# A fused Mamba/MLP mixer layer: the last quarter of the shift and scale sum moved from TensorE to VectorE, and h written by ScalarE

## The chip, the core and the metric

The kernel runs on one core of a Trainium2 chip. The metric is the device time of one execution in microseconds (us); lower is better. The kernel before takes 989.76 us, the median of three runs (989.73 to 990.02).

## The reference

The layer mixes 256 latent tokens, after 256 context tokens, in a width of 2048. What matters here is its beginning: two vectors of conditions, `c` for the latent tokens and `c_ctx` for the context, are multiplied by the large matrix `w_ada`, and the results shift and scale the normalised tokens ahead of the input projection.

```python
sc = jax.nn.silu(c); scc = jax.nn.silu(c_ctx)
shift, scale, gate = jnp.split(sc @ w_ada[l] + b_ada[l], 3, axis=-1)
shift_c, scale_c, gate_c = jnp.split(scc @ w_ada[l] + b_ada[l], 3, axis=-1)
hc = _rmsnorm(ctx, g_pre[l]) * (1.0 + scale_c) + shift_c
zc = hc @ w_in[l][:, :XBC_W + DT_W]
hx = _rmsnorm(x, g_pre[l]) * (1.0 + scale[:, None]) + shift[:, None]
zx = hx @ w_in[l]
```

Everything after that (a convolution, two state-space scans, a gated MLP, the output projection) is the same in both kernels.

## The kernel before, in words

The 2048 channels are 16 tiles of 128 partitions, and `xT` holds all 512 tokens (256 context, 256 latent) along the free axis. h, the normalised, scaled and shifted input, is needed as two halves, `hhi` (rounded to TensorE's fp32r format) and `hlo` (the rest), and each weight likewise as `hi_st` and `lo_st`; a product then takes three matmuls (`mm3`, lines 141 to 143).

**The first stage** ends at about 130 us. It runs 16 rows, one for each channel tile `kt` (line 451). Row `kt` multiplies h of tile `kt` by the weights of seven output tiles and of dt, and sums into PSUM banks that stay open over all rows. A row begins with the matmul of `psdt` by `hhi` (line 418); its fourth matmul group needs `hlo`. While TensorE runs row `kt`, the other engines make what row `kt`+1 needs: the weights' halves (`split_hi` on ScalarE, L352; `split_dt` and `split_lo` on VectorE, L356 and L360) and h itself.

**Shift and scale.** `w_ada` comes in chunks of 1 MB. Tiles 0 to 3 are single units of two chunks; tiles 4 to 15 are six units of two tiles and four chunks each. For a unit `ada_mm` runs 16 matmuls of 128 columns a chunk (L249), in exact fp32, which the profile shows as two records a matmul, so 128 records for four chunks. `ada_fin` transposes the sum (VectorE, L257), and `ada_ab` makes ha = (1 + scale) g and hb = shift, four numbers a partition (ScalarE, L262 and L264).

**h.** `make_h` works on 128x256 halves, context and latent apart: VectorE multiplies x by ha and by `rb`, the row of 1/rms (L365, two instructions), ScalarE adds hb and rounds into `hhi` (L368, two), VectorE forms `hlo` (L370, two).

**What sets the order.** Loads go out on SP's queue in program order; chunks take six buffers in turn, so the load of chunk c+6 waits for the reader of chunk c. The order of TensorE, VectorE, ScalarE and GpSimd in this stage is written by hand: `row_steps` returns a list of steps for a row ("m" a group of matmuls, "a" a chunk, "f" `ada_fin`, "h" `make_h`, "c", "d", "l" the three parts of the weights' split), and each engine runs its instructions in that order. From row 6 on, an odd row ends with h of the next tile behind "f", and an even row begins with the splits and h of the next.

**Ahead of the rows** the sum of x squared for the 1/rms is formed as the four loads of x land: ScalarE and VectorE square tiles in turn (L315, L313), TensorE sums them (L317), with matmuls on ones between them that fill time (`warm`, L305). The sum is transposed (L325), becomes `rb` (L333), and row 0 follows.

Of the kernel before, what the change touches and what calls it, by code (L numbers as in the profile page):

```python
# [15 lines left out]
P = 128  # L16
# [12 lines left out]
NSING = 4  # L29

# [14 lines left out]
def tile_hybrid_ssd_mlp(  # L45
# [66 lines left out]
    def tri(pool, name, sgn, strict):  # L112
# [69 lines left out]
    nc.sync.dma_start(sc2, ccols)  # L182

# [49 lines left out]
    def ada_one(u):  # L233
        pt = ada_ps.pop(u)[1]
        nc.scalar.activation(ha[:, u, :], pt[:, 0:2], AF.Identity, bias=bsc1[:, u : u + 1],
                             scale=pc[:, C_GPRE + u : C_GPRE + u + 1])
        nc.scalar.activation(hb[:, u, :], pt[:, 2:4], AF.Identity, bias=pc[:, C_BADA + u : C_BADA + u + 1])

    def ada_mm(ci):
# [5 lines left out]
        for kk in range(nk):  # L245
            k = k0 + kk
            for g in range(4):
                o = (kk * 4 + g) * n
                nc.tensor.matmul(ps[32 * g : 32 * g + 32, 0:n], lhsT=sc[:, k, :], rhs=raw[:, o : o + n],  # L249
                                 start=k == 0, stop=k == KT - 1)  # L250

    def ada_fin(u):

        ps = ada_ps.pop(u)
        n = 64 * len(UNITS[u])
        ada_ps[u] = tr = st2.tile([P, 128], F32, tag="row", name=f"adat{u}")
        nc.vector.transpose(tr[:, 0:n], ps[:, 0:n])  # L257
        ada_ab(u, 0)

    def ada_ab(u, q):  # L260
        kt, tr = UNITS[u][q], ada_ps[u]
        nc.scalar.activation(ha[:, kt, :], tr[:, 64 * q : 64 * q + 2], AF.Identity, bias=bsc1[:, kt : kt + 1],  # L262
                             scale=pc[:, C_GPRE + kt : C_GPRE + kt + 1])
        nc.scalar.activation(hb[:, kt, :], tr[:, 64 * q + 32 : 64 * q + 34], AF.Identity,  # L264
                             bias=pc[:, C_BADA + kt : C_BADA + kt + 1])
# [31 lines left out]
    nc.scalar.activation(sc[:, :, 0:2], sc2, AF.Silu)  # L297
    nc.scalar.activation(sc2[:, 0, 0:1], epsc, AF.Sqrt)
# [11 lines left out]
    for k in range(KT):  # L310
        sq = yseg((1, 2, 3, 6, 0, 4, 5)[k % 7])
# [6 lines left out]
        if g == 3:  # L318
            warm(512)
            if k < 12:  # L320
                warm(256)
# [39 lines left out]

    def make_h(kt):
        sl = (slice(256, 512), slice(0, 256))
        for v, s in enumerate(sl):
            nc.vector.scalar_tensor_tensor(xT[:, kt, s], xT[:, kt, s], ha[:, kt, v : v + 1], rb[:, s],  # L365
                                           op0=ALU.mult, op1=ALU.mult)
        for v, s in enumerate(sl):
            nc.scalar.activation(hhi[kt][:, s], xT[:, kt, s], AF.Identity, bias=hb[:, kt, v : v + 1])  # L368
        for v, s in enumerate(sl):
            nc.vector.scalar_tensor_tensor(hlo[kt][:, s], xT[:, kt, s], hb[:, kt, v : v + 1],  # L370
                                           hhi[kt][:, s].bitcast(F32), op0=ALU.add, op1=ALU.subtract)
# [9 lines left out]
    def row_steps(kt):  # L381
# [10 lines left out]
        s_ = [("c", n), ("d", n), ("l", n)]  # L392

        a = [("a", c) for c in range(2 * kt + 2, min(2 * kt + 6, 2 * KT))] if n >= NSING and kt % 2 else []
        f = [("f", (n - NSING) // 2 + NSING)] if kt % 2 else []
        f2 = [("f2", (n - NSING) // 2 + NSING)] if kt % 2 else []
        c_, d_, l_, h_ = s_ + [("h", n)]
        if n < NSING:
            r = [("r", 2 * n), ("r", 2 * n + 1)]
            g = m[4:5] + [("g", n), ("o", n), h_]  # L400
            if n < 3:
# [927 lines left out]
```

## Time and profile before

| what | value |
|---|---|
| median of three runs | 989.76 us (989.73 to 990.02) |
| profiled execution, span from first to last instruction | 987.9 us |
| TensorE matmuls busy over the span | 978.8 us, 99% |
| VectorE busy | 621.4 us, 63% |
| ScalarE busy | 495.4 us, 50% |
| granted TensorE clock, mean | 0.999 |
| data moved | 207.26 MB, 210 GB/s over the span |

The profiled execution's span is 1.9 us shorter than the median time of the runs; the rest lies around the span. A profile row of a group reads: line, engine, operation, output<-inputs, shapes, count | busy us, mean ns of one | idle before and what ended it. A row of the timeline reads: start, us, engine, line, operation, shapes, count, and in brackets how long the engine sat idle before it and what ended that. Line numbers in profile rows are those of the kernel before.

### The profile page before, as it was taken

How to read it: one execution, taken by the hardware profiler on the slowest of the kernel's cores; microseconds unless marked ns; L12 is line 12 of the kernel's file. 1: busy time of each engine (PE TensorE's matmuls, PEld its weight loads, DVE VectorE, ACT ScalarE, POOL GpSimd, SP SyncE). 2: the span in 40 equal slices, each digit the busy share in tenths (PEclk: the TensorE clock that was granted, in tenths of full speed). 3: DMA queues.
4: the chain of work that ended last, by engine and by line, in shares of the span. 5: the costliest groups of instructions: out<-in, count | busy, mean ns of one | idle time of the engine just before them, and what ended most of it. 6: DMA issues, size and time to landing. Idle time of an engine off the chain costs nothing.

```text
span 987.9 us, 13929 instructions
## 1 busy us (share of the span) xinstructions
PE 978.8 (99%) x5502; PEld 792.6 (80%) x5502; DVE 621.4 (63%) x949; ACT 495.4 (50%) x762; POOL 112.5 (11%) x162
## 2 busy tenths in 40 slices
PE   9999999999999999999999999999999999999997
PEld 4688888778887878787888888887888888888885
DVE  4444488868886566756767766767555564445636
ACT  4233358566665554545445343454565563346522
POOL 0000002432453222224000000000000000000000
PEclk9999999999999999999999999999999999999999
DMA  9999844233323424145877768774455446556722
GB/s 372 421 418 418 352 149 166 86 129 128 128 75 139 142 98 145 43 169 206 297 302 284 275 257 296 280 274 170 170 180 203 171 170 213 178 206 228 282 86 85
DMA packets 31985, 207.26 MB, mean 210 GB/s; under 512 B 4128, under 2 KB 4384, under 8 KB 8496
## 3 DMA queue, kind: packets, MB, share of 16 engines
q1 hardware_dynamic: 29232, 192.79, 52.0%
q0 software_dynamic: 2112, 12.65, 3.7%
q8 instruction: 43, 0.70, 0.3%
q10 hardware_dynamic: 576, 0.94, 0.3%
q14 instruction: 22, 0.18, 0.1%
HBM read 204.20 MB, written 2.16 MB: 209 GB/s over the span
## 4 chain that ended last, share of the span: by engine, by line
PE 92%; DMA 4%; ACT 2%; DVE 1%; SPq 0%; issue 0%; ACTq 0%
PE pa L1108 12%; PE pa L1110 12%; PE pa L1109 12%; PE psx L141 9%; PE psx L143 9%; PE psx L142 9%; PE pm L1157 3%; PE pm L1155 3%; PE pm L1156 3%; DMA wst<-in_wst_dram 3%; PE pq L1157 2%; PE pq L1156 2%; PE pq L1155 2%; PE psada L249 2%; PE psc L778 1%; PE pso L831 1%
## 5 line engine op out<-in xcount | busy, mean ns | idle before, releaser
L85 DVE TENSOR_TENSOR lo_w<-w,hi_w 128x1024 fp32r<-128x1024 f32 x173 | 210.7, 1224 | 146.0 <-ACT hi_w L84 145.9
L84 ACT CAST hi_w<-w 128x1024 fp32r<-128x1024 f32 x173 | 182.1, 1053 | 204.5 <-PE pa L1110 129.4
L1108 PE MATMUL pa<-hi_w,hhi 128*128 128x512 f32 x512 | 202.3, 395 | 0.0
L1110 PE MATMUL pa<-hi_w,hlo 128*128 128x512 f32 x512 | 199.5, 390 | 0.0
L1109 PE MATMUL pa<-lo_w,hhi 128*128 128x512 f32 x512 | 199.3, 389 | 0.0
L141 PE MATMUL psx<-hhi,hi_w 128*128 128x512 f32 (+1 forms) x400 | 153.4, 383 | 0.0
L143 PE MATMUL psx<-hhi,lo_w 128*128 128x512 f32 (+1 forms) x400 | 145.9, 365 | 0.0
L142 PE MATMUL psx<-hlo,hi_w 128*128 128x512 f32 (+1 forms) x400 | 145.7, 364 | 0.0
L1108 PEld LDWEIGHTS pa<-hi_w,hhi 128*128 128x128 f32 x512 | 96.2, 188 | 20.5 <-issue 1.6
L1110 PEld LDWEIGHTS pa<-hi_w,hlo 128*128 128x128 f32 x512 | 96.1, 188 | 20.3
L1109 PEld LDWEIGHTS pa<-lo_w,hhi 128*128 128x128 f32 x512 | 96.2, 188 | 19.5 <-issue 0.2
L576 DVE SCALAR_TENSOR_TENSOR xbc<-psx,pc,xbc 128x248 f32<-128x248 f32 (+1 forms) x204 | 83.6, 473 | 34.8 <-ACT xbc L560 33.9
L501 DVE TENSOR_TENSOR lo_w<-w,hi_w 128x1024 fp32r<-128x1024 f32 x61 | 77.1, 1271 | 23.7 <-ACT hi_w L495 23.6
L141 PEld LDWEIGHTS psx<-hhi,hi_w 128*128 128x128 f32 x400 | 75.5, 189 | 13.4 <-issue 2.9
L143 PEld LDWEIGHTS psx<-hhi,lo_w 128*128 128x128 f32 x400 | 75.4, 188 | 12.5
L142 PEld LDWEIGHTS psx<-hlo,hi_w 128*128 128x128 f32 x400 | 75.6, 189 | 12.2 <-issue 1.7
L495 ACT CAST hi_w<-w 128x1024 fp32r<-128x1024 f32 x61 | 63.5, 1044 | 26.0 <-PE psx L142 12.9
L966 DVE SCALAR_TENSOR_TENSOR junk<-gate,cb 128x2048 bf16<-128x2048 f32 x16 | 36.7, 2291 | 24.1 <-DMA gate<-in_wada_dram 24.1
L1155 PE MATMUL pm<-hi_w,hhi 128*128 128x512 f32 x128 | 50.0, 390 | 0.0
L1156 PE MATMUL pm<-lo_w,hhi 128*128 128x512 f32 x128 | 49.9, 390 | 0.0
L1157 PE MATMUL pm<-hi_w,hlo 128*128 128x512 f32 x128 | 49.7, 389 | 0.0
L730 ACT ACTIVATE R<-R,y 128x128 f32<-128x128 f32 x128 | 38.8, 391 | 0.0
(248 smaller groups left out, 1333.6 us busy)
## 6 DMA issues: line engine op xcount, KB each, us to landing
w<-in_wlat_dram SPq DMA_DIRECT2D x64, 1024.0 KB, 4.8
w<-in_wout_dram SPq DMA_DIRECT2D x32, 1024.0 KB, 4.8
ada<-in_wada_dram SPq DMA_DIRECT2D x30, 1024.0 KB, 13.4
w<-in_wxbc_dram SPq DMA_DIRECT2D x25, 1024.0 KB, 4.8
gate<-in_wada_dram SPq DMA_DIRECT2D x16, 1024.0 KB, 5.5
R<-acs POOLq DMA_DIRECT2D x8, 1024.0 KB, 5.2
wst<-in_wst_dram SPq DMA_DIRECT2D x15, 480.0 KB, 14.0
xT<-in_xch_dram SPq DMA_DIRECT2D x4, 1024.0 KB, 8.0
```

Source lines behind the costliest of these rows:

```text
L84: nc.scalar.copy(hi, raw)
L85: nc.vector.tensor_tensor(lo, raw, hi.bitcast(F32), op=ALU.subtract)
L141: nc.tensor.matmul(ps, lhsT=whi, rhs=hhi[k][:, s], start=start, stop=False)
L142: nc.tensor.matmul(ps, lhsT=whi, rhs=hlo[k][:, s], start=False, stop=False)
L143: nc.tensor.matmul(ps, lhsT=wlo, rhs=hhi[k][:, s], start=False, stop=stop)
L576: nc.vector.scalar_tensor_tensor(ao, zi, cw[:, k : k + 1], ao, op0=ALU.mult, op1=ALU.add)
L1108: nc.tensor.matmul(pa[tk], lhsT=hhi[k][:, t], rhs=whi[:, w], start=k == 0, stop=False)
L1109: nc.tensor.matmul(pa[tk], lhsT=hhi[k][:, t], rhs=wlo[:, w], start=False, stop=False)
L1110: nc.tensor.matmul(pa[tk], lhsT=hlo[k][:, t], rhs=whi[:, w], start=False, stop=k == KT - 1)
L1155: nc.tensor.matmul(p, lhsT=yh[:, t], rhs=whi[:, w], start=j == 0, stop=False)
L1156: nc.tensor.matmul(p, lhsT=yh[:, t], rhs=wlo[:, w], start=False, stop=False)
L1157: nc.tensor.matmul(p, lhsT=yl[:, t], rhs=whi[:, w], start=False, stop=hf == 0 and j == 15)
```

## The change

For tiles 4 to 15 the last quarter of the sum over the 2048 rows of `w_ada` (`KD` = 12: tiles 12 to 15 of k) is no longer a matmul. The first chunk of each unit is now laid out with the output channels on the partitions, and `ada_part` multiplies its four rows of 512 numbers (shift or scale, of two tiles) by c and by c_ctx, spread over the partitions, with an accumulated sum (eight instructions of 128x512 a unit). The spread rows `cb` are made in the prologue: `crw` is loaded on ScalarE's queue, goes through Silu, is spread by two matmuls with ones in place of two `warm` matmuls, and is copied out of PSUM by ScalarE. `ada_bias` adds the constants; `ada_fin` now writes scale+1 and shift at once with one VectorE addition, so that the four small ScalarE instructions a unit go.

h is made in another way: `scale_x` forms x g /rms ahead of time (VectorE, one 128x512 instruction), `make_h` is four ScalarE instructions of 128x256, two into `hhi` and two that write the exact h back into `xT`, and `make_hl` subtracts (VectorE, one of 128x512). `XROW` says in which row which tile is scaled ahead.

```diff
+KD = 12
+XROW = ((3, 4), (5, 6), (7,), (8, 9), (10, 11), (12, 13), (14, 15))
...
+    crw = wp["raw"].tile([P, 2048], F32, tag="raw", name="crw")[0:1, 0:1024].rearrange("o (v k) -> o v k", v=2)
+    nc.scalar.dma_start(crw, crow[:, KD * P :].unsqueeze(0))
+    cb, cbj = (yseg(2), yseg(3)), yseg(0)
...
-                                 start=k == 0, stop=k == KT - 1)
+                                 start=k == 0, stop=k == (KT if u < NSING else KD) - 1)
+    def ada_part(u, i):
+        q, v = divmod(i, 2)
+        if i == 0:
+            part[u] = ada_raw.pop(4 * u - 2 * NSING), st2.tile([P, 4, 2], F32, tag="part", name=f"part{u}")
+        raw, acc = part[u]
+        nc.vector.scalar_tensor_tensor(cbj, raw[:, q * 512 : (q + 1) * 512], 1.0, cb[v], op0=ALU.mult, op1=ALU.mult,
+                                       accum_out=acc[:, q, v : v + 1])
...
-        ada_ab(u, 0)
+        m = UNITS[u][0]
+        b = part.pop(u)[1] if u in part else bc(bab[:, m], 2, 2)
+        nc.vector.tensor_tensor(hab[:, m : m + n // 64].rearrange("p k q v -> p (k q) v"),
+                                tr[:, 0:n].rearrange("p (q r) -> p q r", r=32)[:, :, 0:2], b, op=ALU.add)
...
+    nc.scalar.activation(crw, crw, AF.Silu)
...
-        if g == 3:
+        if k in (3, 7):
+            v = k // 4
+            pcv = acp.tile([P, 512], F32, tag="acc", name=f"pscb{v}")
+            nc.tensor.matmul(pcv, lhsT=ones[0:1, :], rhs=crw[:, v], start=True, stop=True)
+            nc.scalar.copy(cb[v], pcv)
+        elif g == 3:
             warm(512)
...
+    def scale_x(kt):
+        nc.vector.scalar_tensor_tensor(xT[:, kt, :], xT[:, kt, :], pc[:, C_GPRE + kt : C_GPRE + kt + 1], rb,
+                                       op0=ALU.mult, op1=ALU.mult)
     def make_h(kt):
         sl = (slice(256, 512), slice(0, 256))
+        for t in (hhi[kt], xT[:, kt, :]):
+            for v, s in enumerate(sl):
+                nc.scalar.activation(t[:, s], xT[:, kt, s], AF.Identity, bias=hab[:, kt, 1, v : v + 1],
+                                     scale=hab[:, kt, 0, v : v + 1])
+    def make_hl(kt):
+        nc.vector.tensor_tensor(hlo[kt], xT[:, kt, :], hhi[kt].bitcast(F32), op=ALU.subtract)
...
-        return s_ + a + f + [h_] + f2 + m
+        if kt % 2 == 0:
+            v = [("v", (u + 1, i)) for i in range(4)] if n + 1 < KT else []
+            return [c_, d_, l_, h_, e_] + v + x + m
+        v = [("v", (u, i)) for i in range(4, 8)] + [("b", u)]
+        a = [("a", c) for c in range(p + 1, p + 4)]
+        if n == NSING:
+            return m[:3] + a[:2] + m[3:5] + a[2:] + [c_, d_, l_] + v + [("f", u), h_, e_] + x + m[5:]
+        return a[:1] + m[:4] + a[1:] + [c_] + v + [d_, l_, ("f", u), h_, e_] + x + m[4:]
```

**How the order moves: VectorE, from the unit of tiles 10 and 11 on** (rows 9 to 11 of the stage; `hhi_127` and `hlo_143` are tile 10, `hhi_128` and `hlo_144` tile 11; `lo_st` is the low half of a row's weights). Before:

```order
L257 STREAM_TRANSPOSE adat_1061<-psada_996 128x128 [waits PE_49]
L365 SCALAR_TENSOR_TENSOR xT<-xT,ha,y 128x256 [waits Activation_49]
L365 SCALAR_TENSOR_TENSOR xT<-xT,ha,y 128x256
L370 SCALAR_TENSOR_TENSOR hlo_143<-xT,hb,hhi_127 128x256 [waits Activation_49] x2
L356 TENSOR_TENSOR hi_st_1102<-wst_989,hi_st_1102 128x64 [waits DMAHW1_49,Activation_49]
L360 TENSOR_TENSOR lo_st_1103<-wst_989,hi_st_1102 128x896
L365 SCALAR_TENSOR_TENSOR xT<-xT,ha,y 128x256 x2
L370 SCALAR_TENSOR_TENSOR hlo_144<-xT,hb,hhi_128 128x256 [waits Activation_49] x2
```

Now, on the same engine from the same transpose to the next unit's:

```order
L276 STREAM_TRANSPOSE adat_1051<-psada_981 128x128 [waits PE_49]
L279 TENSOR_TENSOR hab<-adat_1051,part_947 128x8 [waits DVE_49]
L395 TENSOR_TENSOR hlo_143<-xT,hhi_127 128x512 [waits Activation_49]
L377 TENSOR_TENSOR hi_st_1077<-wst_979,hi_st_1077 128x64 [waits DMAHW2_49,Activation_49]
L381 TENSOR_TENSOR lo_st_1078<-wst_979,hi_st_1077 128x896
L395 TENSOR_TENSOR hlo_144<-xT,hhi_128 128x512 [waits Activation_49]
L263 SCALAR_TENSOR_TENSOR y,part_1087<-ada_975,y 128x512 [waits DMAHW0_49]
L263 SCALAR_TENSOR_TENSOR y,part_1087<-ada_975,y 128x512 [waits DVE_49] x7
L269 TENSOR_TENSOR part_1087<-part_1087,bab 128x8 [waits DVE_49]
L377 TENSOR_TENSOR hi_st_1181<-wst_1075,hi_st_1181 128x64 [waits DMAHW5_49,Activation_49]
L381 TENSOR_TENSOR lo_st_1182<-wst_1075,hi_st_1181 128x896 [waits PE_49]
L276 STREAM_TRANSPOSE adat_1191<-psada_1121 128x128 [waits PE_49]
```

The products with x are gone from here, the low half of h stands straight behind the addition that makes shift and scale and waits for ScalarE, and eight accumulated products, each waiting for the one before, stand between the second low half and the next unit's transpose.

**ScalarE at the same place.** Before:

```order
L262 ACTIVATE ha<-adat_1061,bsc_112,pc 128x2 [waits DVE_49]
L264 ACTIVATE hb<-adat_1061,pc 128x2
L368 ACTIVATE hhi_127<-xT,hb 128x256 [waits DVE_49,Activation_49]
L368 ACTIVATE hhi_127<-xT,hb 128x256 [waits DVE_49]
L262 ACTIVATE ha<-adat_1061,bsc_112,pc 128x2
L264 ACTIVATE hb<-adat_1061,pc 128x2
L352 CAST hi_st_1102<-wst_989 128x960 [waits DMAHW1_49,PE_49]
L368 ACTIVATE hhi_128<-xT,hb 128x256 [waits DVE_49,Activation_49]
L368 ACTIVATE hhi_128<-xT,hb 128x256 [waits DVE_49]
```

Now:

```order
L391 ACTIVATE hhi_127<-xT,hab 128x256 [waits DVE_49]
L391 ACTIVATE hhi_127<-xT,hab 128x256
L391 ACTIVATE xT<-xT,hab 128x256 [waits Activation_49] x2
L373 CAST hi_st_1077<-wst_979 128x960 [waits DMAHW2_49,PE_49]
L391 ACTIVATE hhi_128<-xT,hab 128x256 x2
L391 ACTIVATE xT<-xT,hab 128x256 [waits Activation_49] x2
```

The small instructions are gone, each tile has four of 128x256 in place of two, and the weights' cast of the next row stands between the two tiles' h.

**ScalarE in the prologue** (L315 before and L331 now square a tile of x; `pscb` is the spread c in PSUM). Before:

```order
L297 ACT_TABLE_LOAD [waits DMAHW1_49]
L297 ACTIVATE sc<-sc_161 128x16x2 [waits DVE_49]
L298 ACT_TABLE_LOAD
L298 ACTIVATE sc_161<-epsc 128x1 [waits Activation_49]
L315 ACTIVATE y<-xT 128x512 [waits DMAHW2_49]
L315 ACTIVATE y<-xT 128x512
L315 ACTIVATE y<-xT 128x512 [waits DMAHW3_49]
```

Now:

```order
L312 ACT_TABLE_LOAD [waits DMAHW1_49]
L312 ACTIVATE sc<-sc_161 128x16x2 [waits DVE_49]
L313 ACTIVATE crw<-crw 1x1024 [waits DMAHW2_49]
L314 ACT_TABLE_LOAD
L314 ACTIVATE sc_161<-epsc 128x1 [waits Activation_49]
L331 ACTIVATE y<-xT 128x512 [waits DMAHW3_49]
L331 ACTIVATE y<-xT 128x512
L338 COPY y<-pscb_210 128x512 [waits PE_49]
L331 ACTIVATE y<-xT 128x512 [waits DMAHW4_49]
L331 ACTIVATE y<-xT 128x512 [waits DVE_49]
L338 COPY y<-pscb_222 128x512 [waits PE_49]
```

A Silu of 1024 numbers stands ahead of the first square, and a copy that waits for TensorE stands behind the squares of each of the first two loads, ahead of those of the next.

More of the change, by code (lines that the diff above doesn't have):

```diff
@@ L234, in ada_one @@
         pt = ada_ps.pop(u)[1]
[L235 to L237 removed]
+        for q in range(2):
+            nc.scalar.activation(hab[:, u, q, :], pt[:, 2 * q : 2 * q + 2], AF.Identity, bias=bab[:, u, q : q + 1])
     def ada_mm(ci):
@@ L391, in row_steps @@
         n = kt + 1
[L392 to L397, printed above, removed]
+        c_, d_, l_, h_, e_ = [(w, n) for w in ("c", "d", "l", "h", "e")]
+        u = (n - NSING) // 2 + NSING
+        x = [("x", k) for k in XROW[kt]] if kt < len(XROW) else []
+        p = 4 * u - 2 * NSING
         if n < NSING:
@@ L444, in tile_hybrid_ssd_mlp @@
     split_hi(0, 0, WH)
+    scale_x(0)
     ada_fin(0)
```

62 lines of the change are left out of this document (27 added, 35 removed).

## The prediction

> **What bounds the kernel now.** I read the page first, then the stretches between row starts, then the order of events in one pair of rows. From the page, the busy time of each engine:
>
> ```profile
> PE 978.8 (99%) x5502; PEld 792.6 (80%) x5502; DVE 621.4 (63%) x949; ACT 495.4 (50%) x762; POOL 112.5 (11%) x162
> ```
>
> TensorE is full and VectorE (DVE) is not, over the whole span; the change lies in the first stage, so the stretches carry the argument. Each one below runs from the start of an even row of the first stage to the start of the next even row (rows 4, 6, 8, 10, 12, 14). Columns: stretch, length, busy us (and count) of TensorE, weight loads, VectorE, ScalarE, GpSimd, granted clock, share of the DMA engines, GB/s.
>
> ```profile
> 54.54:68.00 13.46, 13.41 (x176) 11.03 (x175) 6.50 (x15) 4.62 (x11) 0.00 (x0) 1.00 1.02 416
> 68.00:81.20 13.20, 13.20 (x174) 11.39 (x175) 6.60 (x15) 5.26 (x12) 0.00 (x0) 1.00 1.02 420
> 81.20:94.30 13.10, 13.10 (x177) 11.30 (x176) 6.12 (x13) 4.85 (x10) 0.00 (x0) 1.00 1.02 417
> 94.30:107.39 13.09, 13.09 (x176) 11.29 (x175) 6.12 (x13) 4.85 (x10) 0.00 (x0) 1.00 1.01 419
> 107.39:120.48 13.09, 13.09 (x176) 11.29 (x175) 6.40 (x15) 5.74 (x11) 0.00 (x0) 1.00 0.74 293
> ...
> 130.00:160.00 30.00, 30.00 (x151) 24.63 (x150) 26.39 (x55) 18.92 (x37) 1.21 (x2) 1.00 0.41 143
> ```
>
> TensorE sets the pace: it has no idle time and a pair of rows takes 13.1 us. DMA is full beside it (416 to 420 GB/s until the loads run out), VectorE is half idle. The last row is the time behind the stage, where TensorE is full as well, so what the stage gains or loses is passed on. Less work on TensorE pays only while VectorE's queue, with its own waits in it, turns round faster than TensorE does. How that queue stands from the middle of one pair to the middle of the next (the unit of tiles 8 and 9), ScalarE (ACT) and VectorE by time, rows between left out:
>
> ```profile
> 88.41 0.99 ACT L352 CAST hi_st<-wst 128x960 fp32r<-128x960 f32 x1 [2.49 <-DMA wst<-in_wst_dram]
> 90.58 0.31 DVE L257 STREAM_TRANSPOSE adat<-psada 128x128 f32<-128x128 f32 x1
> 90.92 0.39 ACT L262 ACTIVATE ha<-adat,bsc,pc 128x2 f32<-128x2 f32 x1 [1.52 <-DVE adat L257]
> 91.22 0.28 ACT L264 ACTIVATE hb<-adat,pc 128x2 f32<-128x2 f32 x1
> 91.92 0.91 ACT L368 ACTIVATE hhi<-xT,hb 128x256 fp32r<-128x256 f32 x2 [0.43 <-DVE xT L365]
> ...
> 95.57 0.23 DVE L356 TENSOR_TENSOR hi_st<-wst,hi_st 128x64 fp32r<-128x64 f32 x1 [2.21 <-ACT hi_st L352]
> 95.71 1.09 DVE L360 TENSOR_TENSOR lo_st<-wst,hi_st 128x896 fp32r<-128x896 f32 x1
> 96.71 0.88 DVE L365 SCALAR_TENSOR_TENSOR xT<-xT,ha,y 128x256 f32<-128x256 f32 x2
> ```
>
> Starts show the pitch, the time from one start to the next: the low half of the weights ends at 96.80 but its successor starts at 96.71, 1.00 after it; two activations of 0.50 take 0.91. An instruction that waits for nothing starts 0.08 to 0.09 us before its forerunner's end.
>
> **Removed from TensorE.** A unit's four chunks take from 72.81 to 76.44, 3.63 us:
>
> ```profile
> 72.81 3.70 PE L249 MATMUL psada<-ada,sc 128*32 128x128 f32 x128
> 76.44 0.50 PE L418 MATMUL psdt<-hhi,hi_st 128*128 128x512 f32 x1
> ```
>
> A quarter is 0.91 us, for six units 5.45 us. Five units now run in two blocks instead of one; I estimate 0.2 us for a border between block and row (the first matmul behind the block has 0.50 against 0.40 us elsewhere, and as much on the way in), so 1.0 us comes back. Net 4.45 us less, and TensorE alone could do a pair in about 12.4 us.
>
> **Added to VectorE.** The nearest rows to the new product are the gate's (same form, accumulated, 2048 columns, with the read of its sum) and a chain of 256 columns in which each instruction waits for the last:
>
> ```profile
> L966 DVE SCALAR_TENSOR_TENSOR junk<-gate,cb 128x2048 bf16<-128x2048 f32 x16 | 36.7, 2291 | 24.1 <-DMA gate<-in_wada_dram 24.1
> L622 DVE SCALAR_TENSOR_TENSOR y<-y 128x256 f32<-128x256 f32 x6 | 2.5, 425 | 0.2
> ```
>
> ```profile
> 134.41 2.72 DVE L622 SCALAR_TENSOR_TENSOR y<-y 128x256 f32<-128x256 f32 x6
> 630.64 2.29 DVE L966 SCALAR_TENSOR_TENSOR junk<-gate,cb 128x2048 bf16<-128x2048 f32 x1 [2.28 <-DMA gate<-in_wada_dram]
> 632.86 0.08 DVE L966 DVE_READ_ACCUMULATOR junk<-gate,cb 128x1 f32 x1
> 644.38 0.17 DVE L975 TENSOR_TENSOR gate<-gate,pc 128x16 f32<-128x16 f32 x1
> ```
>
> Between 256 and 2048 columns a column costs (2.291-0.425)/1792 = 1.04 ns, so 512 columns take 0.69 us. The chain's pitch is (2.72-0.425)/5 = 0.46, 0.03 over its duration. The read of the sum ends at 632.94, 0.01 after its product. One product: 0.73 us (low end 0.69, no gap; high end 0.81, the read's 0.08 in full). Eight a unit: 5.84. The two small additions go by the gate's addition, 0.17+0.03 = 0.20 each.
>
> The Trainium skill speaks against such products: its "Vector Engine (DVE) Microarchitecture Reference", section "Points that are easy to get wrong", says that this instruction runs at half throughput with two SBUF sources that are not bf16. The gate's row has just that, two f32 sources, and its 1.04 ns a column is that of the plain subtractions; the trace does not bear the rule out. By it eight products would cost 4.3 us more a unit; it is a rival below.
>
> x and the low half of h, now 512 columns wide, by rows of that width; h by the rows of an activation with both operands taken from a column of memory:
>
> ```profile
> L1040 DVE SCALAR_TENSOR_TENSOR vt<-vt,rr,gvb 128x512 f32<-128x512 f32 x8 | 5.7, 750 | 4.0 <-DMA gvb<-in_gv_dram 4.0
> L360 DVE TENSOR_TENSOR lo_st<-wst,hi_st 128x512 fp32r<-128x512 f32 x4 | 2.7, 684 | 0.0
> L368 ACT ACTIVATE hhi<-xT,hb 128x256 fp32r<-128x256 f32 x32 | 14.6, 502 | 14.8 <-DVE xT L365 14.8
> L560 ACT ACTIVATE xbc<-psx,pc 128x256 f32<-128x256 f32 x7 | 3.9, 561 | 4.7 <-PE psx L143 4.7
> ```
>
> Pitches: x 0.67, the low half 0.60. An activation with bias and scale: 0.56 by the second (low end 0.50, bias alone; high end 0.61, since scale added 0.11 between L264 and L262), pitch 0.47; four take 3x0.47+0.56 = 1.97.
>
> **VectorE's loop.** It now waits for ScalarE with everything queued behind it. Take t = 0 as the end of an even tile's h on ScalarE. ScalarE casts the next row's weights (0.90) and makes the odd tile's h: done at 0.04+0.90+1.97 = 2.91. VectorE meanwhile subtracts the low half (0.64), does the split (0.14+1.00 behind the cast, from 95.57 to 95.71 to 96.71), stands at the odd tile's low half until 2.95, leaves it at 3.55, then products 5.84 (9.39), bias 0.20 (9.59), split 1.14 (10.73), transpose 0.31 (11.04), addition 0.20 (11.24), and ScalarE needs 0.05+1.97 for the next even tile: **13.26 us a pair**. Where four tiles are scaled ahead in the loop (two pairs, rows 4 to 8), 4x0.67 = 2.68 come in, of which 1.17 fill VectorE's waits: 14.77. VectorE's loop is longer than TensorE's 12.4 in both, so TensorE waits, first for h and then for its low half. Waiting behind these on VectorE are the splits and the next unit's products; SP's loads wait behind the products for their buffer, but run ahead of a slower stage.
>
> **The front.** The prologue as it stands, and a row for each kind that is new there (a copy out of PSUM, an activation of 1024 columns):
>
> ```profile
> 6.17 1.15 ACT L315 ACTIVATE y<-xT 128x512 f32<-128x512 f32 x2
> 6.17 1.29 DVE L313 TENSOR_TENSOR y<-xT 128x512 f32<-128x512 f32 x2 [2.83 <-DMA xT<-in_xch_dram]
> 11.08 1.56 PE L305 MATMUL psw<-ones 128*128 128x512 f32 x4
> 12.57 1.14 PE L317 MATMUL pss<-y,ones 128*32 128x512 f32 x8
> 15.13 1.07 PE L317 MATMUL pss<-y,ones 128*32 128x512 f32 x8
> 30.81 0.50 PE L418 MATMUL psdt<-hhi,hi_st 128*128 128x512 f32 x1 [0.63 <-ACT hhi L368]
> L699 ACT COPY xk<-ptx 128x512 f32<-128x512 f32 x16 | 9.3, 584 | 21.9 <-PE ptx L695 21.9
> L743 ACT ACTIVATE E<-E 128x1024 f32<-128x1024 f32 x8 | 8.5, 1060 | 2.6 <-DVE E L737 2.6
> ```
>
> The Silu of 1024 costs 0.97 (L743) ahead of the first square, which starts at 7.14. The squares end at 8.3, their sums at 8.9, the spread matmul (two thirds of the filler's 1.49 from 11.08 to 12.57) at 9.9, and ScalarE, which waits for it, copies (0.49) and starts the second load's squares at 10.4. The same again puts the third load's at 13.7 and the fourth's at 14.8; the third's sums end at 15.45, filler 1.49, the last sums 1.07, end 18.0 instead of 16.2: 1.8 us later. Behind it scaling tile 0 (0.67) replaces the small instructions. Row 0's low half comes 1.9 to 2.0 late; the 0.63 us that row 1 waits today go, but its own low half comes late by as much. I carry 2.0, and 0.3 for rows 2 and 3. The load of c on ScalarE's queue and the two instructions that set up the constants cost nothing: VectorE idles 2.83 us ahead of the first square, and the load has until the Silu of sc ends on ScalarE; only a load that lands later than that would cost more.
>
> **Row 3 to row 4.** Row 3's matmuls of two columns and what follows:
>
> ```profile
> 42.72 0.61 PE L230 MATMUL psada<-sel,adac 128*128 128x2 f32 x4
> 45.71 0.40 PE L418 MATMUL psdt<-hhi,hi_st 128*128 128x512 f32 x1
> 46.41 0.40 PE L418 MATMUL psdt<-hlo,hi_st 128*128 128x512 f32 x1
> ```
>
> With 2.3 more the small matmuls end at 45.6, two small activations (0.5) and h (1.97) at 48.15. From there VectorE does the low half 0.60, tile 7's x 0.67, products 2.92, split 1.14, products 2.92, bias and transpose and addition 0.71, and two activations 1.08: row 4 starts at 58.2 instead of 54.54, 3.7 late with the 2.3 in it. The same wait once more at the end, which no loop holds: row 14's low half is ready 2x0.47+0.04+0.68 = 1.66 after its first matmul, TensorE asks for it after 0.70 (45.71 to 46.41), so 1.0 is lost there.
>
> **Sum.** Row 4: +3.7. Rows 4 to 8: 2x14.77 = 29.5 against 26.7, +2.9. Rows 8 to 14: 3x13.26 = 39.8 against 39.3, +0.5. Tail: +1.0. Together **+8.1 us**. Behind the stage everything shifts. The profiled span of 987.9 becomes 996.0; the median lies 1.9 above its span, so 989.8 becomes 997.9. Ends: products at 0.81 instead of 0.73 in six units +3.8, activations at 0.61 +1.6: 1003.3; products at 0.69 -1.9, activations at 0.50 -2.2, half the front -1: 992.8.
>
> **Rivals.** (1) VectorE keeps up, because the waits for ScalarE fall into time that TensorE needs anyway: then 4.45 goes and only the front's 2.0 stays, 987.3. For it: summed durations, 5.84+2x(1.08+0.23)+2x0.68+0.71 = 10.5, fit into 12.4. Against it: the order puts the low half straight behind the addition, with 1.97 of ScalarE between. It decides where the two waits together fall below 1.9 us. Chance 0.09. (2) Gains and costs cancel: loops of 12.4 without x and 13.8 with it, and a front of 1: 990. Chance 0.04. (3) Products at half throughput: 6x4.3 = 26 more, 1024. Against it the gate's row. Chance 0.03. My forecast, VectorE's loop as the bound: 0.84.
>
> **How the numbers follow.** A measurement of this kernel tells 0.2%, 2.0 us, from no change. The forecast and its ends lie above that, so slower is 0.84+0.03, faster 0.09, same 0.04. The range is the forecast's own, 992 to 1004.
>
> **What would show it.** In the changed profile, between the starts of rows 4 and 14: VectorE busy over 80%, TensorE with idle time of about 1 to 2.4 us a pair put down to h on ScalarE and to the low half on VectorE, pairs of 14.8 and then 13.3 us, row 4 at 58.2, and VectorE idle only at the low halves. The last sums of squares should end near 18.0. It is wrong if TensorE shows no idle time there and pairs of 12.4 us (then rival 1), or if a product takes 1.2 us (rival 3).

## The result, and the profile after

The changed kernel takes 1002.76 us (median of 4 runs, 1002.12 to 1006.31), the kernel before 989.82 (989.73 to 990.02) beside it: ratio 1.0137, 95% interval 1.0121 to 1.0153. The profiled execution spans 1001.2 us, against 987.9: 13.3 more. The engines over the whole span, from the changed kernel's page:

```profile
PE 980.1 (98%) x5310; PEld 787.3 (79%) x5310; DVE 649.5 (65%) x1027; ACT 507.4 (51%) x771; POOL 112.5 (11%) x162
```

TensorE (PE) has fewer instructions and about the same busy time, so the 13 us are time in which it stands still or runs at a lower clock. Where they arise, from the starts of the rows' first matmuls (psdt<-hhi, L418 before, L443 after), in us:

| row | 0 | 1 | 2 | 3 | 4 | 6 | 8 | 10 | 12 | 14 | 15 |
|---|---|---|---|---|---|---|---|---|---|---|---|
| before | 22.00 | 30.81 | 38.31 | 45.71 | 54.54 | 68.00 | 81.20 | 94.30 | 107.39 | 120.48 | 125.10 |
| after | 26.84 | 35.36 | 43.85 | 51.66 | 61.78 | 76.40 | 91.03 | 106.26 | 119.60 | 132.94 | 138.34 |
| later by | 4.84 | 4.55 | 5.54 | 5.95 | 7.24 | 8.40 | 9.83 | 11.96 | 12.21 | 12.46 | 13.24 |

More than half is there at row 4; from row 15 on nothing is added. The same stretches as before, each a pair of rows (rows 4, 6, 8, 10, 12):

```profile
61.78:76.40 14.62, 13.11 (x143) 10.27 (x143) 12.20 (x29) 5.83 (x11) 0.00 (x0) 1.00 0.94 357
76.40:91.03 14.63, 13.11 (x143) 10.27 (x143) 12.21 (x29) 5.83 (x11) 0.00 (x0) 1.00 0.93 354
91.03:106.26 15.23, 14.48 (x143) 11.49 (x143) 9.90 (x25) 6.17 (x11) 0.00 (x0) 0.89 0.85 314
106.26:119.60 13.34, 12.83 (x145) 10.21 (x143) 9.91 (x25) 5.94 (x11) 0.00 (x0) 1.00 0.99 380
119.60:132.94 13.34, 12.83 (x145) 10.21 (x143) 9.90 (x25) 5.94 (x11) 0.00 (x0) 1.00 0.45 166
```

VectorE (DVE, the fourth figure behind the stretch) was busy for 6.1 to 6.6 us of a pair before; now it is busy for 12.2 of 14.6 us in the first two pairs and for 9.9 of 13.3 in the last two. The third row has a granted clock of 0.89, which the forecast did not have. TensorE's longest wait in the rows is the one ahead of row 4, for h:

```profile
61.78 0.50 PE L443 MATMUL psdt<-hhi,hi_st 128*128 128x512 f32 x1 [1.66 <-ACT hhi L391]
```

One turn of VectorE's queue, with ScalarE (ACT) and TensorE where it waits for them, rows between left out:

```profile
115.54 1.95 PE L254 MATMUL psada<-ada,sc 128*32 128x128 f32 x64
117.56 0.32 DVE L276 STREAM_TRANSPOSE adat<-psada 128x128 f32<-128x128 f32 x1
117.91 0.17 DVE L279 TENSOR_TENSOR hab<-adat,part 128x8 f32<-128x8 f32 x1
118.11 1.09 ACT L391 ACTIVATE hhi<-xT,hab 128x256 fp32r<-128x256 f32 x2 [5.15 <-DVE hab L279]
119.11 1.08 ACT L391 ACTIVATE xT<-xT,hab 128x256 f32<-128x256 f32 x2
120.22 0.69 DVE L395 TENSOR_TENSOR hlo<-xT,hhi 128x512 fp32r<-128x512 f32 x1 [2.15 <-ACT xT L391]
120.97 0.50 PE L443 MATMUL psdt<-hlo,hi_st 128*128 128x512 f32 x1 [0.51 <-DVE hlo L395]
123.09 0.69 DVE L395 TENSOR_TENSOR hlo<-xT,hhi 128x512 fp32r<-128x512 f32 x1 [0.76 <-ACT xT L391]
123.70 0.68 DVE L263 SCALAR_TENSOR_TENSOR y<-ada,y 128x512 f32<-128x512 f32 x1
130.90 0.32 DVE L276 STREAM_TRANSPOSE adat<-psada 128x128 f32<-128x128 f32 x1
```

From transpose to transpose VectorE needs 130.90 - 117.56 = 13.34, of which 2.15 and 0.76 are waits for ScalarE. But the sums on TensorE end at about 117.5 too (115.54 + 1.95), just ahead of the transpose: TensorE's own order could set these 13.34 as well. The experiments take the two apart.

### The profile page after: what moved, and what is told of

Read it like the earlier page. It is cut to its first block, busy times and chain, and to the rows that moved or that the text cites. A ratio compares the mean times of both kernels' runs of the same rounds, so it can differ in the third digit from the quotient of the medians.

```text
span 1001.2 us, 13637 instructions
## 1 busy us (share of the span) xinstructions
PE 980.1 (98%) x5310; PEld 787.3 (79%) x5310; DVE 649.5 (65%) x1027; ACT 507.4 (51%) x771; POOL 112.5 (11%) x162
## 4 chain that ended last, share of the span: by engine, by line
PE 89%; DVE 5%; ACT 4%; issue 1%; DMA 1%; ACTq 0%; DVEq 0%
PE pa L1137 12%; PE pa L1138 12%; PE pa L1139 12%; PE psx L143 9%; PE psx L145 8%; PE psx L144 8%; PE pm L1186 3%; PE pm L1185 3%; PE pm L1184 3%; PE pq L1185 2%; PE pq L1186 2%; PE pq L1184 2%; DVE y L263 2%; PE psc L807 1%; PE pso L860 1%; ACT hhi L391 1%
## 5 line engine op out<-in xcount | busy, mean ns | idle before, releaser
L145 PEld LDWEIGHTS psx<-hhi,lo_w 128*128 128x128 f32 x400 | 75.4, 188 | 12.5
L144 PEld LDWEIGHTS psx<-hlo,hi_w 128*128 128x128 f32 x400 | 75.6, 189 | 12.2 <-issue 1.7
L391 ACT ACTIVATE hhi<-xT,hab 128x256 fp32r<-128x256 f32 x32 | 17.5, 594 | 47.1 <-DVE hab L279 47.0
```

The costliest lines, as they stand in the source:

```text
L144: nc.tensor.matmul(ps, lhsT=whi, rhs=hlo[k][:, s], start=False, stop=False)
L145: nc.tensor.matmul(ps, lhsT=wlo, rhs=hhi[k][:, s], start=False, stop=stop)
```

## The experiments

All are edits of the changed kernel; the diffs show the lines that matter, `...` stands for what is left out, and those of e11, e9 and e12 are shown against the run that they build on. Times are medians; a granted clock is the mean over one execution's span, unless a stretch is named.

### The front

The prologue of the changed kernel; the Silu of c's row is the first line:

```profile
6.41 1.06 ACT L313 ACTIVATE crw<-crw 1x1024 f32<-1x1024 f32 x1 [1.95 <-DMA crw<-in_crow_dram]
7.49 1.28 ACT L314 ACT_TABLE_LOAD   x1
8.89 1.13 ACT L331 ACTIVATE y<-xT 128x512 f32<-128x512 f32 x2
9.55 1.57 PE L333 MATMUL pss<-y,ones 128*32 128x512 f32 x8 [3.15 <-ACT y L331]
12.21 0.59 ACT L338 COPY y<-pscb 128x512 f32<-128x512 f32 x1 [2.19 <-PE pscb L337]
12.70 1.15 ACT L331 ACTIVATE y<-xT 128x512 f32<-128x512 f32 x2
16.52 2.44 ACT L331 ACTIVATE y<-xT 128x512 f32<-128x512 f32 x4
20.20 1.07 PE L333 MATMUL pss<-y,ones 128*32 128x512 f32 x8
```

c's row was asked for at 1.26 and is there at 6.4; ScalarE waits 1.95 us for it ahead of every square. Behind its Silu, in ScalarE's queue, stands the second table load (ACT_TABLE_LOAD, 1.28 us). In the kernel before, that ran ahead of the landing of x (6.17) and cost nothing:

```profile
4.56 1.28 ACT L298 ACT_TABLE_LOAD   x1
```

So the first square starts at 8.89 (before 6.17), 2.7 us late, with the Silu and the table load in sum, though x is there at 6.23 (VectorE squares its tiles from then on). A load's worth of squares then takes 3.81 (8.89, 12.70, 16.52), and the sums end at 21.27 (before 16.20).

**e1_front** builds the spread rows from the columns that are through Silu already, and copies behind the last square:

```diff
-    nc.scalar.dma_start(crw, crow[:, KD * P :].unsqueeze(0))
...
-    nc.scalar.activation(crw, crw, AF.Silu)
...
+    for v in range(2):
+        nc.vector.tensor_tensor(cb[v].rearrange("p (k n) -> p k n", k=KT - KD), bc(ident, 1, KT - KD),
+                                bc(sc[:, KD:KT, v], 2, P), op=ALU.mult)
...
-            nc.tensor.matmul(pcv, lhsT=ones[0:1, :], rhs=crw[:, v], start=True, stop=True)
-            nc.scalar.copy(cb[v], pcv)
+            nc.tensor.matmul(pcb[v], lhsT=ones, rhs=cb[v], start=True, stop=True)
...
+    for v in range(2):
+        nc.scalar.copy(cb[v], pcb[v])
```

> Only the prologue is changed: no load of c as a row and no Silu of it; VectorE lays c's columns (already through Silu) on a diagonal, the two matmuls with ones spread them in the same places, and ScalarE copies both results out behind its last square. Theory A (the front cost 4.6 us because c landed late and the copies stood between the squares, and everything behind it only shifted): the last sums of squares end at 16.2 to 16.8, row 1 starts at 30.8 to 31.4 instead of 35.36, row 4 at 57 to 58, total 998.4 (997.5 to 999.5). Theory B (the front was hidden by the loads or by VectorE's queue in rows 1 to 4, which makes up for an earlier start): row 4 starts at 60.5 or later, total above 1001.

999.59 us, ratio to before 1.0094 (1.0079 to 1.0109). Row 0 starts at 21.81, row 1 at 30.32 and row 3 at 46.65, each 5.0 us earlier than in the changed kernel, as theory A has it (row 1 is even a little ahead of its window). Row 4 starts at 58.15, just behind its window, as the total is: of the 5.0 us, 1.4 are lost again there. VectorE and ScalarE at that place:

```profile
50.34 0.69 DVE L261 SCALAR_TENSOR_TENSOR y<-ada,y 128x512 f32<-128x512 f32 x1
51.27 0.99 ACT L374 CAST hi_st<-wst 128x960 fp32r<-128x960 f32 x1 [4.43 <-DMA wst<-in_wst_dram]
52.30 0.23 DVE L378 TENSOR_TENSOR hi_st<-wst,hi_st 128x64 fp32r<-128x64 f32 x1 [1.25 <-ACT hi_st L374]
53.44 0.69 DVE L261 SCALAR_TENSOR_TENSOR y<-ada,y 128x512 f32<-128x512 f32 x1
```

The weights of row 4 land at 51.27, and the second four products stand behind their split in VectorE's queue though their data is there. So each theory holds for a part: 3.6 us of the front reach row 4.

**e11_copies_between** is e1_front with the two copies back between the squares:

```diff
             nc.tensor.matmul(pcb[v], lhsT=ones, rhs=cb[v], start=True, stop=True)
+            nc.scalar.copy(cb[v], pcb[v])
...
-    for v in range(2):
-        nc.scalar.copy(cb[v], pcb[v])
```

> As e1_front (no load of c as a row, no Silu of it), but the two copies out of PSUM stand between ScalarE's squares again, as in the changed kernel. It splits the front's 5.0 us. If the late load of c and the Silu behind it are about 1.75 and the copies the rest: the first squares start at 6.1, the last sums end at 18.5 to 19.0, row 0 starts at 24.0 to 24.5 (changed kernel 26.84, e1_front 21.81). If the load alone is the cost and the copies fit: row 0 at 22.0 to 22.5. If the copies alone are: 25.0 or later. The total stands between e1_front and the changed kernel by less than row 0 does, as row 4 also waits for its weights: 998.5 to 1001.

1000.25 us (ratio 1.0103, 1.0089 to 1.0116). Row 0 starts at 24.23, inside the first window: the late load, with its Silu and the table load that it pushes back, is 26.84 - 24.23 = 2.6, the copies 24.23 - 21.81 = 2.4. No run takes the load and the Silu apart, and why the load landed only at 6.4 was not tested.

### Who sets the pair

**e2_fill** moves three of the next unit's products into VectorE's wait:

```diff
-            v = [("v", (u + 1, i)) for i in range(4)] if n + 1 < KT else []
+            v = [("v", (u + 1, i)) for i in range(3, 4)] if n + 1 < KT else []
...
-        ... [("f", u), h_, e_] + x + m[4:]
+        ... [("f", u), h_] + [("v", (u + 1, i)) for i in range(3)] + [e_] + x + m[4:]
```

> Only VectorE's order is changed: the first three products of the next unit stand between the addition that finishes a unit and the low half that waits for ScalarE. Theory A (the loop is long because VectorE stands still for 2.15 us at that low half with its whole queue behind it): its loop falls to about 12.5 us in rows 4 to 8 and 11.2 behind, TensorE sets the pace again with pairs of 12.6 to 12.8, row 8 starts near 87 and row 14 near 125 instead of 132.94; total 995 to 997. Theory B (the eight products are too much beside the splits in any order): pairs stay at 13.3 and above, total above 1001.

Neither fits as a whole. Rows 4 to 8 fall from 29.25 to 27.00 (61.45 to 88.45), so the wait was the bound there; but behind row 8 pairs stay at 13.34. There VectorE now stands still elsewhere, 2.23 us ahead of the transpose, for TensorE's last sum; its own loop is then 13.34 - 2.23 = 11.1, as theory A had it:

```profile
113.09 0.32 DVE L276 STREAM_TRANSPOSE adat<-psada 128x128 f32<-128x128 f32 x1 [2.23 <-PE psada L254]
```

Median 1002.62 (ratio 1.0124, 1.0089 to 1.0158), lowest 998.41; its runs scatter to 1005.98 (last section).

**e3_one_product** leaves out seven of the eight products of a unit, so that a part of the sum over c is missing; in `ada_part`:

```diff
+            nc.vector.memset(part[u][1], 0.0)
         raw, acc = part[u]
+        if i:
+            return
```

> Leaves out seven of the eight products of each unit (their sums are set to zero), so a quarter of the sum over c is missing for tiles 4 to 15; all else, loads too, is the changed kernel. It shows what TensorE alone needs with three chunks, and what h through ScalarE costs without a full VectorE. Theory A (products and the wait together make VectorE the bound): pairs of 12.5 to 12.8 in rows 4 to 14, total 994 to 996.5, and no dip of the granted clock between 80 and 130 us. Rival C (the step from the addition through four activations to the low half sets the pair, products or not): TensorE still waits for h 0.8 us and for the low half 0.7 us in each pair, pairs above 13.1, total above 998.

996.95 us (ratio 1.0068, 1.0051 to 1.0085), between the totals of both theories, and pairs of 13.33: neither the 12.5 of theory A nor rival C's wait for h. VectorE is idle for nearly 6 us of the pair, and yet TensorE waits for the low half (TensorE, VectorE and ScalarE by time, rows between left out):

```profile
85.65 1.96 PE L254 MATMUL psada<-ada,sc 128*32 128x128 f32 x64
87.53 0.39 PE L143 MATMUL psx<-hhi,hi_st 128*128 128x256 f32 x1
87.67 0.32 DVE L279 STREAM_TRANSPOSE adat<-psada 128x128 f32<-128x128 f32 x1 [3.60 <-PE psada L254]
88.22 1.10 ACT L394 ACTIVATE hhi<-xT,hab 128x256 fp32r<-128x256 f32 x2 [6.08 <-DVE hab L282]
89.73 0.40 PE L446 MATMUL psdt<-hhi,hi_st 128*128 128x512 f32 x1
90.34 0.69 DVE L398 TENSOR_TENSOR hlo<-xT,hhi 128x512 fp32r<-128x512 f32 x1 [2.15 <-ACT xT L394]
91.09 0.50 PE L446 MATMUL psdt<-hlo,hi_st 128*128 128x512 f32 x1 [0.49 <-DVE hlo L398]
```

This is a loop of TensorE with itself. Its last sum ends at 87.6; transpose, addition, four activations and the low half take until 91.0; meanwhile TensorE has only four matmul groups, two of them half as wide (87.53 to 89.73), and 0.70 us of the next row to do, and stands still at the low half. The change put the second block of sums behind four matmul groups of the row instead of ahead of the row, so that less work covers the chain, and it made the chain longer: from the start of the transpose to the end of the low half it takes 3.36 us (87.67 to 91.03). In the kernel before it was 2.78 (90.58, in the rows of the prediction, to 93.36):

```profile
92.47 0.89 DVE L370 SCALAR_TENSOR_TENSOR hlo<-xT,hb,hhi 128x256 fp32r<-128x256 f32 x2 [0.24 <-ACT hhi L368]
```

**e4_h_alone** keeps the whole sum on TensorE, four chunks a unit, and before's prologue:

```diff
-KD = 12
+KD = 16
...
-        v = [("v", (u, i)) for i in range(4, 8)] + [("b", u)]
-        a = [("a", c) for c in range(p + 1, p + 4)]
+        v = []
+        a = [("a", c) for c in range(p, p + 4)]
```

> The other part alone: x ahead on VectorE, h and its rewrite by ScalarE, the low half as one subtraction, but the whole sum on TensorE again (four chunks a unit) and the prologue of the kernel before. Theory A (beyond the front, h through ScalarE costs 1.4 us in rows 1 to 3 and 0.8 at the end, and nothing between, since TensorE's 13.1 a pair cover it): total 991 to 993. Rival C (h through ScalarE costs its wait in every pair): pairs of 13.5 and more, total 995 or above.

997.62 us (ratio 1.0075, 1.006 to 1.009): rival C. Pairs take 14.2 instead of 13.1, with no product on VectorE at all:

```profile
84.50:98.72 14.22, 13.70 (x177) 11.06 (x176) 4.33 (x8) 5.97 (x12) 0.00 (x0) 1.00 0.96 379
```

VectorE is busy 4.33 us of it. Of the 1.1 us more, 0.5 is time in which TensorE waits (14.22 - 13.70) and 0.6 is more busy time (13.70 against 13.09); the run does not take h and the two blocks apart. So h through ScalarE, with the sums in two blocks, loses 7.5 us, more than the 5.45 us of sums that the shifted quarter takes off TensorE.

**e5_sums_early** lengthens what covers that chain:

```diff
-        return a[:1] + m[:4] + a[1:] + [c_] + ...
+        return a[:1] + m[:2] + a[1:] + m[2:4] + [c_] + ...
```

> Only TensorE's order is changed: in the odd rows from 5 on the second block of sums (two chunks) stands behind two matmul groups of the row instead of four. The run with one product of eight had pairs of 13.33 us with VectorE mostly free, so there TensorE waits for its own chain: last sum, transpose, addition, four activations, low half. Theory A (VectorE's own loop is 13.3 us as forecast, and the two loops are equal by chance): pairs of rows 8 to 14 stay at 13.2 to 13.4 and rows 4 to 8 at 14.6, total within 1 us of the changed kernel without a dip of the clock, 1001 to 1003. Theory D (only TensorE's chain sets the pair, VectorE has room): pairs fall to 12.7 behind row 8 and the total to 999 to 1000.

Theory A. The two pairs from row 10 on:

```profile
104.64:117.86 13.22, 12.86 (x144) 10.21 (x143) 9.82 (x25) 5.94 (x11) 0.00 (x0) 1.00 1.00 394
117.86:131.09 13.23, 12.87 (x144) 10.22 (x143) 9.82 (x25) 5.84 (x11) 0.00 (x0) 1.00 0.45 172
```

With TensorE's loop shortened VectorE's stands alone: 13.23, forecast 13.26. (The pair of rows 8 and 9 took 13.06.) Total 1003.38 (ratio 1.0135, 1.0112 to 1.0158), lowest 1001.13; two of the four executions had a clock of 0.991 and 0.989.

**e6_fill_sums_early** is e2_fill and e5_sums_early together.

> Both orders together: three products of the next unit in VectorE's wait, and TensorE's second block of sums earlier. If both loops bound the pair (theory A with the chain added), pairs fall to 12.6 to 12.8 from row 4 on, TensorE without a wait behind row 4; row 14 starts near 125 instead of 128.5, total 994.5 to 996 without a dip. If something third holds the pair (loads, the weights' split), pairs stay above 13.1 and the total at 998.

```profile
89.00:101.58 12.58, 12.58 (x145) 10.28 (x144) 9.82 (x25) 5.94 (x12) 0.00 (x0) 1.00 1.01 406
```

TensorE is full, pairs take 12.58, and row 14 starts at 126.7 (114.16 + 12.58), 1.7 behind the forecast: the profiled execution has a stretch at half clock behind row 4. Alone, the edits moved the late pairs by 0.0 and 0.1; both together by 0.76. That is what two loops of equal length look like. Median 999.97 (ratio 1.0109, 1.0084 to 1.0133), above the window, which was for executions without a dip of the clock; lowest 995.97.

**e7_rewrite_on_vector** lets VectorE make the unrounded h of single and even tiles in the time in which it waited:

```diff
+        own = kt < NSING or kt % 2 == 0
+        if own:
+            for v, s in enumerate(sl):
+                nc.vector.tensor_scalar(yseg(6)[:, s], xT[:, kt, s], hab[:, kt, 0, v : v + 1], hab[:, kt, 1, v : v + 1],
+                                        op0=ALU.mult, op1=ALU.add)
-        for t in (hhi[kt], xT[:, kt, :]):
+        for t in (hhi[kt],) if own else (hhi[kt], xT[:, kt, :]):
```

> For tiles 0 to 3 and the even tiles VectorE makes the unrounded h itself in another tile (two instructions of 256 columns), while ScalarE makes the rounded one; the low half then waits for two activations instead of four. It shortens the chain by about 1.0 us at each unit's start and VectorE's wait of 2.15 by about 1. Theory A plus the chain: no wait for the low half in rows 1 to 14 (0.75 each in rows 0 and 1, 0.5 to 0.75 in the even rows, today), pairs of 12.7 behind row 8 and 13.5 in rows 4 to 8, row 4 at 60; total 995 to 998. Rival (VectorE's own products hold the pair): only rows 0 to 3 gain, total 1000 to 1001.5.

993.13 us (ratio 1.0038, 1.0024 to 1.0052), a little under the window. Both loops get shorter by one edit: pairs of 13.63 in rows 4 to 8 and 12.54 from row 10 on, and the waits for the low half in rows 0 and 1 are gone.

### All repairs, and what is left then

**e8_all** joins e1_front, e5_sums_early and e7_rewrite_on_vector, and moves steps on VectorE:

```diff
-XROW = ((3, 4), (5, 6), (7,), (8, 9), (10, 11), (12, 13), (14, 15))
+XROW = ((3, 4, 5), (6, 7, 8), (9, 10, 11), (), (12,), (13,), (14,), (15,))
...
-            return [c_, d_, l_, h_, e_] + v + x + m
+            return [c_, d_, l_, h_] + v[:2] + [e_] + v[2:] + x + m
...
-        ... v + [d_, l_, ("f", u), h_, e_] + x + m[4:]
+        ... v + [d_, ("f", u), h_, l_, e_] + x + m[4:]
```

> All repairs together: prologue without the row of c, second block of sums earlier, unrounded h by VectorE for single and even tiles, x scaled three tiles a row in rows 0 to 2, and VectorE's splits of weights moved behind the addition that finishes a unit, two products ahead of the odd tile's low half. If front, chain and VectorE's waits are the whole loss: row 4 at 55.5 to 56.5, pairs of 12.7, row 14 near 119.5, total 987.5 to 990, that is at or under the kernel before. If something else is lost (weights that land too late for row 4, ScalarE's own queue), row 4 stands at 58 and the total above 991.5.

989.48 us, ratio 0.9993 (0.9984 to 1.0003): the whole loss is found, no gain beyond it. One wait of more than 0.6 us is left in the rows, and the clock falls behind it; row 4, and the pair that begins there:

```profile
55.40 0.50 PE L450 MATMUL psdt<-hhi,hi_st 128*128 128x512 f32 x1 [1.66 <-ACT hhi L397]
```

```profile
55.40:70.06 14.66, 14.66 (x143) 11.37 (x144) 12.17 (x31) 5.06 (x8) 0.00 (x0) 0.88 1.03 416
70.06:82.64 12.58, 12.58 (x145) 10.29 (x144) 11.73 (x30) 5.07 (x8) 0.00 (x0) 1.00 1.01 416
```

**e9_x_late** takes the three x of row 2 off that path:

```diff
-XROW = ((3, 4, 5), (6, 7, 8), (9, 10, 11), (), (12,), (13,), (14,), (15,))
+XROW = ((3, 4, 5), (6, 7, 8), (), (9,), (10,), (11,), (12,), (13,), (14,), (15,))
```

> As e8_all, but row 2 scales no x ahead; tiles 9 to 15 are scaled one a row in rows 3 to 9. In e8_all VectorE's eight products for tiles 4 and 5 start behind three such instructions (2.07 us), and TensorE waits 1.66 us at row 4, with the granted clock at 0.58 for 4 us behind it. Theory A (what remains is that queue): products end before the weights of tile 4 are cast, row 4 starts at 54.0 to 54.6 instead of 55.40, TensorE waits under 0.7 us there, the clock stays at 1.00 in rows 4 and 5, row 14 near 117; total 986 to 987.5, under the kernel before by 2.5 to 4. Rival (the loads set row 4, since the cast waits for them until 51.3): row 4 not before 55, total 988.5 or more.

Row 4 starts at 54.23 and the clock stays up, as theory A said, though TensorE still waits 0.84 us there. The total is 988.99 (ratio 0.9990, 0.9980 to 0.9999), above theory A's window and in the rival's, since rows 4 to 8 now take 27.6. There ScalarE's casts wait for the loads:

```profile
57.58 0.99 ACT L374 CAST hi_st<-wst 128x960 fp32r<-128x960 f32 x1 [3.40 <-DMA wst<-in_wst_dram]
63.75 0.99 ACT L374 CAST hi_st<-wst 128x960 fp32r<-128x960 f32 x1 [3.20 <-DMA wst<-in_wst_dram]
```

**e12_weights_first** is e9_x_late with another order on SP's queue:

```diff
-        if kt < NSING - 2:
+        if kt < KT - 2:
             wst_load(kt + 2)
         ada_load(*cs)
-        if NSING - 2 <= kt < KT - 2:
-            wst_load(kt + 2)
```

> As e9_x_late, but in every row the load of the weights stands ahead of that row's two chunks of the matrix for c on SP's queue. In e9_x_late the cast of row 5's weights waits for its load until 57.58 and that of row 6 until 63.75, VectorE waits 2.5 us behind the first, and rows 4 to 8 take 27.6 us instead of 25.2. Theory A (the order of the loads holds those rows; each weight tile is half the size of a chunk and is asked for earlier): the cast of row 5 starts 2 us earlier, rows 4 to 8 take 25.2 to 26, total 986.5 to 988. Rival (the sum of the bytes holds them, DMA moves 416 to 420 GB/s from 2 us on): the chunks land later by as much, rows 4 to 8 still take over 27, total 988.5 to 990.

987.99 us, ratio 0.998 (0.9971 to 0.9989): 1.8 us under the kernel before and 14.8 under the changed one. Row 5's cast starts at 54.05, rows 4 to 8 take 26.67 (54.22 to 80.89), between the two windows: now a chunk of the matrix comes 0.64 us late once:

```profile
63.68 1.08 PE L252 MATMUL psada<-ada,sc 128*32 128x128 f32 x32 [0.64 <-DMA ada<-in_wada_dram]
```

## Why the prediction was right, and which of its terms were off

| term | forecast | measured |
|---|---|---|
| row 4 | +3.7 | +7.24 |
| rows 4 to 8 | +2.9 (2 x 14.77) | +2.59 (2 x 14.63) |
| rows 8 to 14 | +0.5 (3 x 13.26) | +2.63 (15.23, 13.34, 13.34) |
| tail | +1.0 | +0.78 |
| sum | +8.1 | +13.24 |

**Direction and mechanism held.** VectorE's in-order queue, with its wait for ScalarE inside, is longer than TensorE's work. Its turn was forecast at 14.77 and 13.26 and measured at 14.63 and, alone, 13.23 (e5_sums_early). Rival 1 fell: TensorE waits, and e6_fill_sums_early shows what it needed: VectorE's wait of 2.15 us filled and TensorE's sums earlier. Rival 3 fell with the products:

```profile
L263 DVE SCALAR_TENSOR_TENSOR y<-ada,y 128x512 f32<-128x512 f32 x48 | 33.1, 690 | 1.4
L263 DVE DVE_READ_ACCUMULATOR y<-ada,y 128x1 f32 x48 | 3.9, 81 | 0.0
```

0.69 each, next start 0.73 later, with two f32 sources, as forecast; a plain subtraction of 512 columns takes 0.684 (L360 in the prediction). The sentence of the Trainium skill on half throughput ("Vector Engine (DVE) Microarchitecture Reference", "Points that are easy to get wrong") does not hold for this instruction here.

**The term that was most mis-sized is the front.** The step that failed is "the load has until the Silu of sc ends on ScalarE; only a load that lands later than that would cost more". It landed at 6.4 and ended 1.95 us of waiting on ScalarE. The table load behind the Silu was not in the sum either: the first square comes 2.72 later (8.89 against 6.17), not 0.97. I also put the sums' end 1.76 behind the first square; it is 2.2, three times over. Row 0 came 4.84 late instead of 2.0. From row 1 to row 3 the cost is 1.4 more (16.30 against 14.90), not 0.3: row 1 waits 0.74 for its low half and row 2 about 0.3; the rest was not traced. Row 3 to row 4 was right: 1.29 (10.12 against 8.83), forecast 1.4.

**A second loop was missed.** "TensorE alone could do a pair in about 12.4" is 12.58 in its work, as the two blocks of sums and their borders give back 2.4 us (5.45 less six times 0.51, which is 13.09 - 12.58) and not 1.0, and 13.33 in its order (e3_one_product). I followed VectorE's wait round VectorE, but not the chain round TensorE, whose cover the change cut by moving the sums. In the changed kernel the two are equal, so the forecast of rows 12 to 14 is right without showing this; it would have misled anyone who repaired VectorE alone, as e2_fill did.

**The clock was not in the sum.** Of the +2.63 in rows 8 to 14, 15.23 - 13.34 = 1.9 is the pair with the stretch at half clock: 3.4 us at half speed lose 1.7.

**What was luck.** The median lies within 992 to 1004, but 4.9 above the forecast of 997.9, and not for the reasons that gave the upper end. That end stood for products of 0.81 and activations of 0.61; the products came at 0.73, and an activation at 0.59 (four take 2.08, forecast 1.97). The front and the clock, which the upper end did not hold, made the difference. Of the signs that were named, TensorE's idle time is 1.5 us a pair in rows 4 to 8, as forecast, but 0.5 behind row 10; VectorE is busy 54.1 of the 71.2 us between rows 4 and 14, 76% and not over 80%; and the last sums end at 21.27, not at 18.0.

## What to carry to other kernels

When work leaves the full engine for one that looks half idle, lay out a turn of each in-order queue with its waits in it, the full engine's own chain among them: from its last result through the others and back, and what it has to do meanwhile. Two loops can be of equal length; then shortening one of them shows next to nothing, and only both together show that the diagnosis was right. A small load on the path of the prologue is priced by when it lands and by what stands behind it in its engine's queue (here a table load of 1.28 us that was hidden before), not by its size.

## What was not expected of the hardware

**A wait on TensorE can cost twice.** The changed kernel's clock in three stretches around its row 8, where TensorE waited 0.79 and 0.75 us within 2.5 us:

```profile
92.40:92.90 0.50, 0.16 (x1) 0.16 (x2) 0.31 (x2) 0.50 (x2) 0.00 (x0) 1.00 1.05 411
92.90:96.30 3.40, 3.40 (x10) 2.67 (x11) 2.62 (x6) 2.81 (x5) 0.00 (x0) 0.53 1.02 410
96.30:96.80 0.50, 0.50 (x4) 0.50 (x4) 0.50 (x1) 0.00 (x0) 0.00 (x0) 0.81 0.89 377
```

The clock is halved from 93.1 to 96.5, for 3.4 us. Eight of the 14 profiled executions have such a stretch, each of them one, and its length takes two values: 3.4 us in five (this one, e5, e6, e8 and e11) and 6.8, twice as long, in three (e1 from 57.3 to 64.1, e3 from 10.6 to 17.4, e10 from 62.5 to 69.4). The Trainium skill ("TensorE: Matmul & The Clock Gate", "Part 1: The HAM clock gate") has free-running windows of 3.4 us and a clock that is halved behind an idle window; the length agrees. But the waits ahead of this stretch were 0.79 and 0.75 us, and the longest at any of the eight was 2.98 (e1). So the rule of the Trainium skill against gaps over 3.4 us ("TensorE: Matmul & The Clock Gate", "HAM oscillation — how this bites in real kernels") is too mild here. The same waits at row 6 had no dip, nor had those of 1.66 and 0.74 at row 4 and the gap of 3.15 in the prologue of the same execution, so where it falls is open. In e8_all, with a wait of 1.66 us at row 4, 6 of 10 executions had a mean clock of 0.997; in e9_x_late, with 0.84 there, all 11 had 0.998 or 0.999.

Larger dips go with TensorE's gap in the prologue, 3.15 us here and 1.4 to 2.1 in the other profiles. The kernels that have it (the changed one, e2, e3, e5, e6, e7) had a clock under 0.993 in 8 of 26 executions, 4 to 8 us above their own fastest; those without it, in none of 48. Most of the 48 differ in more than the gap; e1, e4 and e11, which keep waits in the pairs, make up 12 of them. One profile shows a dip in the prologue itself, that of e3, behind a gap of 2.05 us:

```profile
10.60:17.40 6.80, 6.75 (x18) 1.37 (x12) 1.48 (x3) 1.63 (x3) 0.00 (x0) 0.50 1.01 414
```

Row 0 starts there at 29.57, 2.7 later than in the changed kernel, and the execution took 1000.47 us, 3.4 to 3.8 more than the other three of that kernel. The direct test, **e10_filled_front**, fills the gap:

```diff
-    warm(512, 512, 512, 512)
+    warm(*[512] * 7)
```

> The changed kernel with three more filler matmuls of 512 columns ahead of the first sums of squares, where TensorE has nothing to do from 6.4 to 9.55. Theory G (the half clock of some executions follows a gap on TensorE; the long gap of the prologue causes the large dips): no execution at a clock under 0.994 and none above 1004.5, median 1001.5 to 1002.5; dips behind row 4's wait can remain (0.995 to 0.998). Rival (dips come by chance, whatever TensorE does): again one execution in three at 0.989 to 0.992 and 1005 to 1006.

All four executions have 0.995 to 0.997 and 1002.75 to 1003.45; median 1002.88 (ratio 1.0131, 1.0117 to 1.0144), 0.4 above the window; the profiled one has a dip behind row 4's wait (clock 0.50 from 62.5 to 69.4). Four executions alone would not exclude chance, and they ran on another chip than e2 to e7; with the 44 others without the gap and the profile of e3 they speak for theory G, without proving it. None of the executions with a clock under 0.993 was profiled, so where those dips lie was not seen.
